# A two-layer mixer and mixture-of-experts kernel on Trainium2: block-ordered tokens at the second layer's hand-over

## The chip, the cores and the metric

One core of one Trainium2 chip runs the whole program in one launch. The metric is device time in microseconds (us), the median of several runs. Engines are named as in the profile: PE is TensorE, DVE is VectorE, ACT is ScalarE, POOL is GpSimd, SP is SyncE, which here only issues DMAs.

## What is computed

Two layers run over 256 tokens and 256 context tokens of width 1024 in float32. Each has a token mixer, an output projection, a layer norm, and a mixture of 16 experts of which every token uses two. In the second layer the context drops out, and only the 256 tokens go through the experts.

```python
y, yc = mixer(h, hc, w_in[l], ...)
x = layer_norm(alpha * x + g1 * y, ln1_g[l], ln1_b[l])
h2 = x * (1.0 + sc2) + sh2
f = moe(h2, w_router, router_bias, w_gate[l], w_up[l], w_down[l])
x = layer_norm(alpha * x + g2 * f, ln2_g[l], ln2_b[l])

def moe(h, ...):
    s = sigmoid(h @ w_router)          # 16 scores a token
    ...                                # best group of four experts, best two in it
    for e in range(16):
        y = y + gates[:, e:e+1] * ((silu(h @ w_gate[e]) * (h @ w_up[e])) @ w_down[e])
```

## The kernel before

Tokens stand on partitions, 128 to a block. In the second layer there are two blocks, `tb` 0 and 1. A row of 1024 features is split for a contraction into 8 groups of 128. The weights are laid out so that feature p * 8 + k lies on partition p in group k; a token's row is therefore seen as `t (p k)`, and group k of it is read in steps of 8 numbers (32 bytes).

**Order of the work.** Each engine has one queue. The build framework fills the queues from the order of the code, from priorities and from data dependences; `behind` and `seq` (a dependence without a semaphore) pin some neighbours by hand, and `hold` names the last instruction of ACT and of DVE behind which later work has to stay. Buffers are rotated: a load waits until the readers of its buffer are done.

**The hand-over of the second layer** lies between the output projection (`outproj`, line 727) and the first expert (`experts1`). These are its steps:
- `ln1` (line 776) takes the projection's sums, adds the residual, and keeps the result in `zs`, with the mean and the reciprocal root of the variance aside. `trans` and `logits` turn `zs` on PE and multiply it by the router's weights. `cent` (line 837) subtracts the mean and multiplies by the row `V["A2"]`; `norm` (line 841) multiplies by the root and adds `V["B2"]`. Their result is `h2`, in tile C. `keep` is true in the second layer: `h2` stays in memory and isn't written out.
- `part` (line 899, called in two steps for each block) splits `h2` into three bf16 pieces `hp` in tile A whose sum is the float32 value: a cast on ACT, the rest on DVE, a second cast on ACT, and the rest of the rest on DVE. In the kernel before, `h2` is ordered `t (p k)` and the pieces `t k p`, so each step reads `h2` in steps of 32 bytes; the first rest overwrites `h2`.
- `score` (line 1365) turns the router's sums into scores (a sigmoid on ACT), ranks them on DVE, and ends in `chb`, the chosen experts as zeros and ones (line 1417). `route` counts them on PE with the constant tiles `tri` and `one` (lines 1434 and 1438), and derives positions; `onehot` (line 1930) makes the selecting matrices `oh`, and `sort` orders the experts by load and writes their numbers, `eid`.
- `hgather` (line 1942) gathers the tokens of the first expert with 48 bf16 matmuls of the pieces and `oh`. ACT copies the result, and then the experts run back to back on PE: `gu` (gate and up), `dn` (down), `acc` (the sum).

The experts' weights come as pieces of 1 MB through SP's queue into a ring of 17 buffers (`wload`, line 1762). For the later experts SP first loads `eid` into registers (`expert`, line 1775). From its first free buffer on, the ring is refilled as PE gives pieces up.

**The modulation rows.** `vectors` (line 656) makes four rows `md`: 0 is g1, 1 is A2, 2 is B2, 3 is g2; ACT writes them to DRAM as `vd` with one DMA, and SP reads them back spread over all partitions (`vload`, line 689) into `V`.

## Time and profile before

| | us |
|---|---|
| median of 3 runs (lowest to highest) | 1177.66 (1174.02 to 1183.37) |
| profiled execution | 1171.57 |
| its span, first to last instruction | 1169.7 |
| PE busy in the span | 1066.6 (91%) |
| DVE busy | 745.1 (64%) |
| ACT busy | 526.5 (45%) |
| POOL busy | 127.7 (11%) |

The profile is of one execution. Its times count from the first instruction. A row of the chain gives a piece of work that the end of the program waited for; a row of the timeline gives every instruction, whether waited for or not; a row of the windows gives for a stretch how long each engine was busy, the clock that TensorE was granted (1.00 is 2.4 GHz, 0.50 is 1.2 GHz) and what the 16 DMA engines moved. "Idle before" is what an engine waited for.

### The profile page before, as it was taken

The numbers are of one execution on the slowest core, as the hardware profiler recorded it, in microseconds if no ns is written. First come the engines' busy times: TensorE is split into PE (matmuls) and PEld (weight loads), VectorE is DVE, ScalarE is ACT, GpSimd is POOL, SyncE is SP. The second block draws the span as 40 slices with busy tenths as digits, with TensorE's granted clock in tenths as the row PEclk, the third lists the DMA queues.
The fourth block names the chain that finished last, engine by engine and source line by source line (L and its number), as shares of the span: only waits on it lengthen the run. The fifth ranks groups of instructions, "written<-read, shape, count | busy, mean of one in ns | idle before, by whom it ended". The sixth has DMA issues, their size and how long they took to land.

```text
span 1169.7 us, 18719 instructions
## 1 busy us (share of the span) xinstructions
PE 1066.6 (91%) x7041; PEld 696.0 (60%) x7041; DVE 745.1 (64%) x1703; ACT 526.5 (45%) x872; POOL 127.7 (11%) x136
## 2 busy tenths in 40 slices
PE   5999999999994999999999868999999499999992
PEld 3766766665684777677543468667657345544441
DVE  3456687768689999788623685678786932222224
ACT  2363443437553778588633454543555511111112
POOL 0000011100000134344320000101100000000000
PEclk9999999999996999999999989999999599999996
DMA  9757666653376899799999941645539389999992
GB/s 378 274 211 260 251 231 234 232 187 145 109 271 213 299 354 360 273 356 392 368 406 415 409 155 72 232 165 180 181 121 344 138 345 423 420 422 423 421 422 96
DMA packets 55202, 327.14 MB, mean 280 GB/s; under 512 B 9467, under 2 KB 9723, under 8 KB 19776
## 3 DMA queue, kind: packets, MB, share of 16 engines
q1 hardware_dynamic: 44080, 275.60, 60.9%
q0 software_dynamic: 9152, 50.10, 11.6%
q8 instruction: 57, 0.93, 0.3%
q10 hardware_dynamic: 1872, 0.16, 0.1%
q14 instruction: 41, 0.34, 0.1%
HBM read 316.53 MB, written 13.09 MB: 282 GB/s over the span
## 4 chain that ended last, share of the span: by engine, by line
PE 49%; DVE 7%; ACT 3%; issue 2%; DMA 1%; POOL 1%; DVEq 0%; ACTq 0%; POOLq 0%
PE gu L185 9%; PE gu L1647 6%; PE proj L432 6%; PE dn L185 4%; PE dn L1647 4%; PE gu L1638 4%; PE hgt L185 2%; PE acc L185 2%; PE dn L1638 2%; PE op L727 2%; DMA G<-in_w_ada_dram 1%; PE hgt L1597 1%; PE S L1117 1%; PE pt L1140 1%; PE py L1147 1%
## 5 line engine op out<-in xcount | busy, mean ns | idle before, releaser
L294 ACT CAST T<-G 128x1024 fp32r<-128x1024 f32 (+2 forms) x79 | 78.1, 994 | 83.9 <-PE proj L432 56.2
L294 ACT CAST S<-G 128x1024 fp32r<-128x1024 f32 (+2 forms) x83 | 79.3, 958 | 79.0 <-PE proj L432 51.5
L304 DVE TENSOR_TENSOR S<-G,S 128x1024 fp32r<-128x1024 f32 (+2 forms) x75 | 85.2, 1140 | 41.4 <-ACT S L294 39.6
L185 PE MATMUL gu<-G,C 128*64 128x512 f32 (+2 forms) x608 | 107.8, 501 | 0.7 <-ACT C L1620 0.7
L304 DVE TENSOR_TENSOR T<-G,T 128x1024 fp32r<-128x1024 f32 (+2 forms) x69 | 82.3, 1198 | 39.7 <-ACT T L294 39.1
L432 PE MATMUL proj<-A,T 128*128 128x512 f32 (+1 forms) x336 | 97.2, 363 | 1.5 <-ACT T L294 1.0
L432 PE MATMUL proj<-A,S 128*128 128x256 f32 (+1 forms) x336 | 88.5, 342 | 1.3 <-DVE S L304 0.9
L1970 DVE SCALAR_TENSOR_TENSOR vt<-dn,slot,con 128x512 f32<-128x512 f32 x17 | 12.8, 751 | 98.6 <-PE dn L185 98.5
L185 PEld LDWEIGHTS gu<-G,C 128*64 128x64 f32 (+2 forms) x608 | 37.6, 128 | 56.7 <-issue 47.5
L432 PEld LDWEIGHTS proj<-A,T 128*128 128x128 f32 x336 | 59.7, 189 | 16.7 <-issue 4.6
L432 PEld LDWEIGHTS proj<-A,S 128*128 128x128 f32 x336 | 58.2, 190 | 11.5 <-issue 3.1
L1971 ACT CAST S<-vt 128x512 fp32r<-128x512 f32 x17 | 10.5, 618 | 98.8 <-DVE vt L1970 98.8
L1647 PE MATMUL gu<-C,A 128*128 128x512 f32 (+3 forms) x180 | 49.7, 408 | 1.2 <-DVE C L304 1.2
L1647 PE MATMUL gu<-T,A 128*128 128x512 f32 (+3 forms) x174 | 47.6, 402 | 3.4 <-POOL T L302 2.2
L404 POOL DMA_DIRECT2D G<-in_w_ada_dram x40 | 21.9, 548 | 258.0 <-PE ada L411 164.7
L185 PE MATMUL dn<-G,A 128*64 128x512 f32 (+2 forms) x224 | 46.8, 594 | 0.4 <-ACT A L1620 0.4
L1590 POOL DMA_INDIRECT G<-h2d,idx x16 | 22.2, 1386 | 216.5 <-DVE oh L1574 138.7
L294 ACT CAST C<-G 128x1024 fp32r<-128x1024 f32 x38 | 39.8, 1047 | 12.8 <-PE gu L1647 8.0
L1129 ACT ACTIVATE G<-G,nm 128x512 f32<-128x512 f32 x48 | 34.4, 718 | 21.3 <-DVE nm L1127 10.8
L1638 PE MATMUL gu<-G,C 128*64 128x512 f32 x192 | 43.0, 595 | 0.0
L989 DVE TENSOR_TENSOR G<-G 128x256 f32<-128x256 f32 x112 | 42.6, 417 | 0.6
L411 PE MATMUL ada<-G,sT 128*32 128x256 f32 x640 | 40.3, 383 | 2.1 <-DMA G<-in_w_ada_dram 2.0
(477 smaller groups left out, 2387.2 us busy)
## 6 DMA issues: line engine op xcount, KB each, us to landing
G<-in_w_gate_dram SPq DMA_DIRECT2D x62, 1024.0 KB, 12.6
G<-in_w_up_dram SPq DMA_DIRECT2D x60, 1024.0 KB, 8.0
G<-in_w_down_dram SPq DMA_DIRECT2D x60, 1024.0 KB, 11.0
G<-in_w_ada_dram POOLq DMA_DIRECT2D x40, 1024.0 KB, 7.6
G<-in_w_in_dram SPq DMA_DIRECT2D x22, 1024.0 KB, 8.7
G<-in_w_out_dram SPq DMA_DIRECT2D x12, 1024.0 KB, 6.7
G<-in_w_ada_dram SPq DMA_DIRECT2D x8, 1024.0 KB, 15.9
G<-vd SPq DMA_DIRECT2D x11, 512.0 KB, 3.8
```

The costliest lines, as they stand in the source:

```text
L185: return self._then(self.b.nc.tensor.matmul(*a, **k))
L294: self.lasts = [self.nc.scalar.copy(hi, raw)]
L304: self.lasts.append(sub(lo, raw, v))
L404: self.late(nc.gpsimd.dma_start(t, self.ap["w_ada"][l, 4 * s + q]))
L411: nc.tensor.matmul(pb[g:g + 32, i * 256:(i + 1) * 256], self.sT[:, kb, :], w[i][:, kb * 256:(kb + 1) * 256], start=kb < 4, stop=kb >= 4, t ...
L432: self.nc.tensor.matmul(pb[:, t], a[:, c], m, start=first and n == 0 and i == 0, stop=last and n == len(kbs) - 1 and i == 2)
L727: nc.tensor.matmul(pbs[tb][h], a, w[j][h], start=n == 0 and i == 0, stop=n == KB - 1 and i == 2)
L989: mul = lambda o, v: tt(o, o, v.to_broadcast([P, n, c]), op=OP.mult)
L1129: nc.scalar.activation(Pt, Pt, AF.Exp, scale=-1.0, bias=m, accum_out=ls[:, i:i + 1])
L1590: self.lastg = nc.gpsimd.indirect_dma_start(out=hg[:cap], out_offset=None, in_=h2d[:, :], in_offset=bass.IndirectOffsetOnAxis(ap=ig, axis= ...
L1638: self.pe.matmul(pb[t], h[0][:, g + i], w[o // PIECE][:, o % PIECE:o % PIECE + 512], start=g == 0, stop=g + m == nk, tile_position=(0, i * ...
L1647: nc.tensor.matmul(pbs[j][:cap], h[a][:, k], ws[b][:, c], start=k == 0 and q == 0, stop=k == nk - 1 and q == 2)
```

## The change

`cent` and `norm` now make `h2` in the order `t (k p)`, block by block: `cent` reads `zs` in steps of 32 bytes and writes a contiguous row. For this the rows A2 and B2 are written to `vd` in that order, row by row (four DMAs from ACT instead of one). `part` then works on contiguous rows; the rest goes into a tile of its own (`rest`, in S) instead of over `h2`, and block 0's last subtraction moves from DVE to GpSimd. The calls of `part` move forward: block 0's second step into `ln1`, block 1's first step behind `norm(1)` in `score`, block 1's second step to the top of `route`. Last, PE gets 18 matmuls of the constant tile `one` (bf16, 512 columns) behind the last router matmul; nothing reads their result.

```diff
--- before.py
+++ after.py
@@ -44,6 +44,7 @@
 SPLITC = 6
 FILLS = ((4, 5, 4, 1), (3, 2, 1, 0))
 EARLY = 6
+WARM = 18
 TAILS = (4, 2)
 BANKS1 = {"gu": "d", "hgt": "d", "dn": "m", "hT": "m", "sl": "m"}
 ACC = "mmmd"
@@ -192,6 +193,12 @@
     def __init__(self, tc, ap, out, dbg=None, caps=CAPS):
         self.pe = tc.nc.tensor
         self.tc, self.nc, self.ap, self.out, self.dbg, self.caps = tc, tc.nc, ap, out, dbg or {}, caps
+
+    def warm(self, n, after):
+        out = self.bank("warm").rearrange("p (a b) -> p a b", a=4)
+        for _ in range(n):
+            i = self.nc.tensor.matmul(out, self.one, self.one[:, None, :].to_broadcast([P, 4, P]), start=True, stop=True)
+            self.behind(i, after)
 
     def dump(self, name, t):
         if name in self.dbg:
@@ -683,8 +690,14 @@
             nc.tensor.matmul(pv[:, :, c], self.onef, rb[:, :, c], start=True, stop=True)
         nc.vector.tensor_copy(self.rb[:, :, :n], pv[:, :, :n])
         self.vd = self.dram([8, D], f"vd{l}")
+        vd = self.vd[:, :].rearrange("(r c) (p k) -> p r c k", c=2, k=KB)
+        if l == DEPTH - 1 and not self.general:
+            turned = self.vd[:, :].rearrange("(r c) (k p) -> p r c k", c=2, k=KB)
+            for r in range(4):
+                nc.scalar.dma_start((turned if r in (1, 2) else vd)[:, r, 0], md[:, r, 0])
+            return
         for c in range(n):
-            nc.scalar.dma_start(self.vd[:, :].rearrange("(r c) (p k) -> p r c k", c=2, k=KB)[:, :, c], md[:, :, c])
+            nc.scalar.dma_start(vd[:, :, c], md[:, :, c])
 
     def vload(self, dst, row):
         self.late(self.nc.sync.dma_start(dst, row.to_broadcast([P, D])))
@@ -830,11 +843,16 @@
 
         def logits(tb, hT):
             for kb in range(KB):
-                nc.tensor.matmul(lg[:, tb * NE:(tb + 1) * NE], hT[:, kb * P:(kb + 1) * P], self.wA[:, c, kb, :],
-                                 start=kb == 0, stop=kb == KB - 1)
+                i = nc.tensor.matmul(lg[:, tb * NE:(tb + 1) * NE], hT[:, kb * P:(kb + 1) * P], self.wA[:, c, kb, :],
+                                     start=kb == 0, stop=kb == KB - 1)
+            return i
 
         def cent(tb):
-            return stt(h2[tb], zs[tb], col(nmu, gs[tb]), V["A2", c], op0=OP.add, op1=OP.mult)
+            o, i, m = h2[tb], zs[tb], V["A2", c]
+            if keep:
+                o, m = (v.rearrange("t (k p) -> t k p", k=KB) for v in (o, m))
+                i = i.rearrange("t (p k) -> t k p", k=KB)
+            return stt(o, i, col(nmu, gs[tb]), m, op0=OP.add, op1=OP.mult)
 
         def norm(tb):
             g = gs[tb]
@@ -853,16 +871,21 @@
             square(1)
             hT1 = trans(1)
             logits(0, hT)
-            logits(1, hT1)
+            i = logits(1, hT1)
+            if keep:
+                self.warm(WARM, i)
             va.append(self.rsqrt(col(vs, 1), col(rstd, gs[1]), roots[1]))
             va.append(cent(1))
             if keep:
                 hp = [self.region("A", F32)[:, j * (D // 2):(j + 1) * (D // 2)].bitcast(BF16).rearrange("t (k p) -> t k p", k=KB)
                       for j in range(6)]
                 self.hp = [hp[0:3], hp[3:6]]
+                r1 = self.region("S", F32)
+                self.rest = [r1[:, j * D:(j + 1) * D] for j in range(2)]
                 a, v = self.part(0, h2[0], 0)
                 aa.append(a)
                 va.append(v)
+                aa.append(self.part(0, h2[0], 1)[0])
             aa.append(nc.scalar.activation(self.st("sg", 1), col(nmu, gs[1]), AF.Sigmoid))
             self.hold = [self.seq(*aa), self.seq(*va)]
         else:
@@ -889,7 +912,12 @@
         if final:
             self.res = res
             self.h2 = h2
-            self.score(l, c, lambda: norm(1))
+            def between():
+                norm(1)
+                if keep:
+                    self.part(1, h2[1], 0)
+
+            self.score(l, c, between)
         else:
             self.score(l, c)
             yield
@@ -897,9 +925,11 @@
         yield
 
     def part(self, tb, h, i):
-        v = h.rearrange("t (p k) -> t k p", k=KB)
+        v, r = (u.rearrange("t (k p) -> t k p", k=KB) for u in (h, self.rest[tb]))
         p = self.hp[tb]
-        return self.nc.scalar.copy(p[i], v), self.nc.vector.tensor_sub(v if i == 0 else p[2], v, p[i])
+        if i == 0:
+            return self.nc.scalar.copy(p[0], v), self.nc.vector.tensor_sub(r, v, p[0])
+        return self.nc.scalar.copy(p[1], r), (self.nc.vector if tb else self.nc.gpsimd).tensor_sub(p[2], r, p[1])
 
     def evict(self, l, c, pb):
         nc = self.nc
@@ -1427,8 +1457,7 @@
         tt = nc.vector.tensor_tensor
         pp = self.bank("pos")
         if l == DEPTH - 1 and not self.general:
-            self.part(0, self.h2[0], 1)
-            self.part(1, self.h2[1], 0)
+            self.part(1, self.h2[1], 1)
         for tb in range(B):
             for o in range(tb + 1):
                 nc.tensor.matmul(pp[:, tb * NE:(tb + 1) * NE], self.tri if o == tb else self.one, chb[:, o],
@@ -1506,7 +1535,6 @@
         posr = self.posr = self.st("posr", 4 * NE, bufs=1)[:, :B * N].rearrange("p (b e) -> p b e", b=B)
         if l == DEPTH - 1:
             self.hold[1] = self.onehot(l, 0)
-            self.part(1, self.h2[1], 1)
             sort()
             gates()
             tt(w[:, 0], w[:, 0], den[:, :, None].to_broadcast([P, B, NE]), op=OP.mult)
```

Line numbers of the changed kernel are some 7 to 30 higher than those of the kernel before.

DVE, from the second `norm` to the comparisons of the ranking. Tile C is `h2`, A the pieces, S the new rest, `vt` and `cmp` scratch of the ranking. Before:

```order
L841 SCALAR_TENSOR_TENSOR C<-C,st_7407,G 128x1024
L1399 TENSOR_TENSOR vt<-rs,s_rbias 128x32
L902 TENSOR_TENSOR A<-C,A 128x1024
L1401 TENSOR_TENSOR vt<-vt 128x8x3
L1402 TENSOR_TENSOR vt<-vt 128x8x2
L1403 TENSOR_TENSOR vt<-vt 128x8
L902 TENSOR_TENSOR C<-C,A 128x8x128
L1404 TENSOR_REDUCE vt<-vt 128x8
L1488 MEMSET vt 128x1 x2
L1409 TENSOR_TENSOR cmp<-vt 128x160
L1410 TENSOR_TENSOR cmp<-vt 128x160
```

After, at the same place:

```order
L859 SCALAR_TENSOR_TENSOR C<-C,st_7410,G 128x1024
L1429 TENSOR_TENSOR vt<-rs,s_rbias 128x32
L1517 MEMSET vt 128x1 x2
L1431 TENSOR_TENSOR vt<-vt 128x8x3
L1432 TENSOR_TENSOR vt<-vt 128x8x2
L1433 TENSOR_TENSOR vt<-vt 128x8
L1517 MEMSET vt 128x1
L1518 MEMSET vt 128x13
L1434 TENSOR_REDUCE vt<-vt 128x8
L1439 TENSOR_TENSOR cmp<-vt 128x160
L931 TENSOR_TENSOR S<-C,A 128x1024
L1440 TENSOR_TENSOR cmp<-vt 128x160
```

Block 0's last subtraction (A<-C,A) is gone from DVE, block 1's first (now S<-C,A) stands one comparison later, and four memsets come earlier.

ACT, from the first cast to the copy of the gathered tokens. The sigmoid of the scores is `rs<-rs`. Before:

```order
L902 CAST A<-C 128x1024
L866 ACT_TABLE_LOAD
L866 ACTIVATE sg<-st_7407 128x1
L902 CAST A<-C 128x1024
L1391 ACTIVATE rs<-rs 128x32
L902 CAST A<-C 128x1024 x2
L1620 COPY C<-hgt 128x512
```

After, at the same place:

```order
L931 CAST A<-C 128x1024
L932 CAST A<-S 128x1024
L889 ACT_TABLE_LOAD
L889 ACTIVATE sg<-st_7410 128x1
L1421 ACTIVATE rs<-rs 128x32
L931 CAST A<-C 128x1024
L932 CAST A<-S 128x1024
L1648 COPY C<-hgt 128x512
```

The second cast of block 0 now stands ahead of the table load and of the scores' sigmoid, where it stood behind both.

SP, in the second layer's mixer (`vd` read as rows g1 and A2). Before:

```order
L266 DMA G<-in_w_in_dram 128x2048 x6
L1771 DMA G<-in_w_gate_dram 128x2048
L266 DMA G<-in_w_in_dram 128x2048
L266 DMA G<-in_w_out_dram 128x2048 x3
L690 DMA G<-vd_6755 128x1024 x2
L266 DMA G<-in_w_out_dram 128x2048
```

After, at the same place:

```order
L273 DMA G<-in_w_in_dram 128x2048 x4
L703 DMA G<-vd_6755 128x1024 x2
L273 DMA G<-in_w_in_dram 128x2048 x2
L1799 DMA G<-in_w_gate_dram 128x2048
L273 DMA G<-in_w_in_dram 128x2048
L273 DMA G<-in_w_out_dram 128x2048 x4
```

The two reads of `vd` are now three loads of `w_in`, three of `w_out` and one of `w_gate` further ahead. In the first layer's output projection some instructions of PE, DVE and ACT change places, though no code of it is changed.

## Rows read from the trace of the kernel before

**Rows 1.** Windows: us; busy us (count) of PE, PEld, DVE, ACT, POOL; clock; DMA share; GB/s.

```profile
909.00:910.00 1.00, 1.00 (x10) 1.00 (x9) 0.96 (x2) 0.21 (x1) 0.00 (x0) 0.87 0.00 0
...
937.00:938.00 1.00, 1.00 (x6) 0.28 (x4) 1.00 (x4) 0.00 (x0) 0.00 (x0) 0.98 0.00 0
...
1000.00:1050.00 50.00, 50.00 (x344) 24.72 (x338) 10.46 (x32) 7.61 (x14) 0.00 (x0) 1.00 1.01 421
```

**Rows 2.** Chain that ended last, from 880 us on: start, us, what.

```profile
905.92 1.28 DVE C L837
...
913.15 2.00 ACT A L902
...
915.18 2.04 DVE C L902
...
928.50 0.18 DVE chb L1417
...
929.72 2.73 PE hgt L1942 x48
...
933.16 8.99 PE gu L185 x32
...
948.29 3.58 PE gu L185 x16
...
958.74 1.51 PE hgt L185 x48
...
1145.78 1.97 PE dn L185 x16
```

**Rows 3.** Timeline of the pause: start, us, engine, line, operation, tiles, shapes [idle].

```profile
905.37 0.39 PE L727 MATMUL op<-T,A 128*128 128x512 f32 x1
...
912.46 3.60 PE L833 MATMUL lg<-wA,B 128*128 128x16 f32 x16
...
912.90 1.28 DVE L837 SCALAR_TENSOR_TENSOR C<-G,st 128x1024 f32<-128x1024 f32 x1
...
915.17 1.28 ACT L866 ACT_TABLE_LOAD   x1
...
917.67 1.29 DVE L841 SCALAR_TENSOR_TENSOR C<-C,st,G 128x1024 f32<-128x1024 f32 x1
...
919.21 0.22 ACT L1391 ACTIVATE rs<-rs 128x32 f32<-128x32 f32 x1
...
919.46 0.19 DVE L1399 TENSOR_TENSOR vt<-rs,s_rbias 128x32 f32<-128x32 f32 x1 [0.49 <-ACT rs L1391]
...
925.80 1.99 DVE L902 TENSOR_TENSOR A<-C,A 128x1024 bf16<-128x1024 f32 x1 [0.96 <-ACT A L902]
```

**Rows 4.** Line 294, casts into S: ns min/median/max, first and last start, forms.

```profile
L294 ACT CAST S<-G x83: 398/1048/1074, 15.3 to 897.2; 128x1024 fp32r<-128x1024 f32 x71, 128x256 fp32r<-128x256 f32 x11, 128x512 fp32r<-128x512 f32 x1
```

**Rows 5.** Timeline of the first layer's experts, DVE and POOL.

```profile
411.72 1.33 POOL L302 TENSOR_TENSOR S<-G,S 128x512 fp32r<-128x512 f32 x1 [1.07 <-ACT S L294]
...
411.83 2.30 DVE L304 TENSOR_TENSOR T<-G,T 128x1024 fp32r<-128x1024 f32 x1
...
414.13 1.21 DVE L304 TENSOR_TENSOR C<-G,C 128x1024 fp32r<-128x1024 f32 x1
```

**Rows 6.** Line 302, GpSimd's subtractions into S.

```profile
L302 POOL TENSOR_TENSOR S<-G,S x8: 1274/1950/2320, 411.7 to 553.8; 128x512 fp32r<-128x512 f32 x8
```

**Rows 7.** SP: the loads of expert numbers, and the first weight load after them.

```profile
L1777 SPq TENSOR_LOAD <-eid x8: 263/268/278, 933.1 to 937.5; - x8
...
938.76 0.34 SPq L1771 DMA_DIRECT2D G<-in_w_down_dram  x1
```

**Rows 8.** DMA issues of 1122 to 1124 us: count, KB each, us to landing.

```profile
G<-in_w_down_dram SPq DMA_DIRECT2D x1, 1024.0 KB, 19.7
```

**Rows 9.** Line 667, the products that make row A2; and w_in loads of 775 to 795 us.

```profile
L667 DVE TENSOR_TENSOR md<-g,s_lnv x2: 166/177/188, 112.1 to 752.8; 128x16 f32<-128x16 f32 x1, 128x8 f32<-128x8 f32 x1
...
L266 SPq DMA_DIRECT2D G<-in_w_in_dram x2: 328/328/328, 776.6 to 791.9; - x2
```

## Prediction

> **What bounds the kernel now.** I read the windows first, then the chain of waits, then the timeline of the stretch in which the chain leaves PE, and last the waits of SP's queue. The chain shows PE nearly everywhere; the exception that this change touches is the pause between the router's matmuls, which end at 912.46 + 3.60 = 916.06 us [rows 3], and the first expert's gate at 933.16 [rows 2]. In it the chain goes through the first centring (905.92), a cast (913.15, 2.00 us), a subtraction (915.18, 2.04), the scores, more casts and subtractions, `chb` (928.50 to 928.68), the gather (929.72, 2.73) and a copy. Every step of the split stands there with about 2.0 us [rows 2, 3]. The clock falls between 909 and 910 (its mean is 0.87: full for 0.74 us, so the fall is at 909.74), 4.0 us after the last projection matmul (905.37 + 0.39 = 905.76), and is back up at 937.0, 3.9 us after the gate began [rows 1 to 3]. The gather takes 2.73 us at 1.2 GHz against 1.51 later at 2.4 GHz, the gate 8.99 for 32 matmuls against 3.58 for 16 [rows 2].
>
> From then on two things run side by side to the end: PE without a gap, and DMA at a share of 1.01 and 421 GB/s [rows 1]. The refill starts late because SP reads eight expert numbers first, from 933.1 to about 938.0 (the last of eight starts at 937.5, 0.6 us apart); its first load goes out at 938.76, when PE also has freed a buffer [rows 7]. At the end the DMA is only just ahead: the last down piece but one, issued at 1122.0, lands 19.7 us later at 1141.7 [rows 8]; the next follows one 2.8 us later (1 MB takes 2.5 us at 421 GB/s), and the matmuls that need it begin at 1145.78, its half about 1 us later [rows 2]. That is some 2.3 us of slack.
>
> **The change, step by step.** I replay the pause from 905.92 with new durations.
>
> The centring now reads in steps of 32 bytes. No row shows this operation so; the bounds are 1.28 us, its present price [rows 2], and 2.04, the dearest strided operation of that size [rows 2]. I take 2.0, since the subtractions of the same size read the same way: +0.7 us on the chain for block 0, and all behind it is late by this. In return a cast falls from 2.0 to 1.05 [rows 4], and a subtraction from 2.0 to 1.21 [rows 5].
>
> Block 0: the cast runs from 913.87 to 914.9. The second centring, 912.90 [rows 3] plus 0.7, ends at 915.6 and is late next; the subtraction follows to 916.8. Before, it ended at 917.2: only 0.4 us are won here. The four small score operations take what they took between 917.2 and 917.67 [rows 3], and `norm(1)` runs 917.3 to 918.6. On ACT the second cast now goes first (916.8 to 917.9), and the table load of 1.28 us [rows 3], which stood hidden under the first subtraction, follows it: the sigmoid ends at 919.5 instead of 919.4. So up to the scores nothing is won at all.
>
> GpSimd's subtraction: its inputs are there at 917.9. The nearest rows are halves of this size, 1.27 to 2.32 us [rows 6]; doubled, 2.5 to 4.6. I take 2.6, twice the uncontended 1.3. What it does to DVE is seen in the first layer: a GpSimd half runs 411.72 to 413.05, and the DVE subtraction that starts at 411.83 takes 2.30 us, not the 1.21 of the next one; it ends 1.08 after GpSimd does [rows 5]. DVE stood still for as long as GpSimd ran. Here GpSimd begins when `norm(1)` lets it, at 918.6, and ends at 921.2; the ranking's first addition (before at 919.46 [rows 3]) is ready at 919.6 and loses 1.6 us. The Trainium skill ("SBUF — State Buffer", section "SBUF: two separate sides") has the rule that speaks against the change: a GpSimd operation and a DVE operation with two SBUF inputs exclude each other for a whole instruction. Rows 5 agree; by the opposite view, that work moved to an idle engine is free, the sum would be 1.6 us better, which is a rival below.
>
> From the addition to the end of `chb` before: 919.46 to 928.68 are 9.2 us, of which three subtractions of 2.0 and a wait of 0.96 for ACT [rows 3] are 6.9; 2.3 are small operations. Now two subtractions remain (2.4), and ACT's cast of 1.05 lies beside the comparisons: 921.2 + 2.3 + 2.4 = 925.9. **`chb` comes 2.8 us sooner.** Positions, `oh` and `eid` keep their order behind it.
>
> The 18 matmuls start at 916.06 + 0.7 = 916.8. No row has their size; 48 matmuls of 64 columns took 2.73 and 1.51 us [rows 2], 57 and 31 ns each, so 512 columns are an estimated 0.46 at 1.2 GHz and 0.25 at 2.4: 4.5 to 8.2 us in all. With the clock up 3.9 us after they begin, it is 3.9 + 2.4 = 6.3, to 923.1; even the upper bound ends at 925.0, before `chb`. They delay nothing. What they bring hangs on the clock holding until the gather at 926.9. The fall before came 4.0 us after dense work [rows 1, 3]; that would be 927.1 here, about the moment when the gather begins, and the rise may come sooner or later than it did at the gate. This is close to a toss-up. I take it that it holds: the gather costs 1.5, not 2.7 (−1.2), the gate begins at 933.16 − 4.0 = 929.2 and takes 7.0 instead of 9.0. PE is then 6.0 us ahead.
>
> The refill gains less. SP needs `eid` (2.8 sooner) and its eight reads, to 935.2; its first load leaves at 935.3, 3.5 us sooner. The weights' stream is full to the end, so its end moves by 3.5, and PE can use that plus the slack of 2.3: 5.8. **The end moves by 5.5 us** (between the two, a little less for small losses).
>
> At nothing I cost the DMAs of `vd`. A2's products are made at 752.8, and the read of A2 now stands on SP ahead of the w_in load of 776.6 [rows 9], so the write has some 20 us to land. In its new order each element is a run of 4 bytes, for which there is no row; if it took longer than that cover, SP's queue would hand each further us to the w_in loads behind the read. The moved instructions in the first layer are the same work in another order on a busy PE: 0, give or take 1.5 us.
>
> Sum: 1171.57 − 5.5 = 1166.1 for an execution like the profiled one. That execution is 6.1 us under the median of 1177.66, so I forecast **1172.2 us**, −0.5%.
>
> **Rivals.**
> - *The clock is down again when the gather comes.* For it: the 4.0 us above; against: the fall before came after a stretch of transposes and small matmuls, not in a free one, so the spacing isn't known well. Then −2.8 remains, PE and refill alike: 1174.9.
> - *DVE isn't held up*, because GpSimd's piece falls between DVE's operations. For it: DVE idles from 918.6 to 919.6; against: rows 5. Then `chb` is 4.4 sooner, PE with the clock 7.6, the refill 4.9 plus slack 7.2: 1170.5.
> - *GpSimd is slow with bf16.* Place: DVE between the scores and the ranking, and the gather, which needs this piece. No row shows GpSimd with bf16 operands. At twice the slowest float32 row, 9.3 us, it ends at 927.9, `chb` at 932.6, 4.0 later than now, the clock is lost again: 1181.7. It decides from 5.4 us of the subtraction on without the clock's gain, from about 8.6 with it. Against: every GpSimd half of this kind took at most 2.32 [rows 6].
> - *The 18 matmuls leave the clock unmoved,* or the clock rises and falls before use: the first rival's number.
>
> **How the numbers follow.** Forecast 0.42, first rival 0.30, second 0.14, third 0.09, the rest (first layer's order, `vd` late) 0.05. All but the third lie below the old median, and all within 1% of it, which is about what a measurement of this kernel can tell from no change. The range holds the first three cases, 1170.5 to 1174.9, and as the three runs of before differ by up to 9 us, 5 us on either side: 1165.5 to 1180. Faster by over 1% would need 11.8 us; the whole pause is 17 us and no sum above gives it without the spread of the runs: 0.10. Slower by over 1% needs more than the third rival or a stall of the queues: 0.04.
>
> **What would show it.** Right: the contiguous casts at 1.05 and subtractions at 1.2; the centring at 2.0; one DVE addition behind the scores stretched until GpSimd's subtraction ends; `chb` about 12.6 us after the router's matmuls before, 9.1 after; the granted clock at 1.00 during the first gather, which takes 1.5; eight register reads, not PE, ahead of the first refill. Wrong: a gather of 2.7 and a gate of 9 (first rival), an addition that isn't stretched (second), a GpSimd piece beyond 5 us (third), PE waiting for weights at the end by more than the shift allows, or a w_in load later than its buffer.

## Result and the profile after

| us | before | after |
|---|---|---|
| median, same chip, 7 runs each | 1174.00 | 1186.66 |
| lowest to highest | 1170.52 to 1183.37 | 1184.89 to 1196.23 |
| profiled execution | 1171.57 | 1196.23 |
| its span | 1169.7 | 1194.2 |

The ratio is 1.0119, with a 95% interval of 1.0097 to 1.0142: about 1.2% slower, where 1172.2 us and a range up to 1180 were forecast. Of the experiments below, one execution of run 9 and one of the kernel before beside it took 2074 and 4524 us and are left out of the ratios. The profiled execution of after is the slowest of its seven, so its rows overstate the loss, by some 10 us against the median.

To find the place, I laid SP's loads of the two profiles side by side, since SP has the same loads in both, but for the earlier place of the two reads of `vd`: a load of `w_in` ahead of the second layer's mixer, the gate load in the middle of its mixer, the gate load at the start of its output projection. Before:

```profile
680.94 111.27 SPq L266 DMA_DIRECT2D G<-in_w_in_dram  x6
803.36 0.33 SPq L1771 DMA_DIRECT2D G<-in_w_gate_dram  x1
...
864.81 0.33 SPq L1771 DMA_DIRECT2D G<-in_w_gate_dram  x1
```


After:

```profile
687.44 75.74 SPq L273 DMA_DIRECT2D G<-in_w_in_dram  x4
778.51 0.82 SPq L703 DMA_DIRECT2D G<-vd  x2
...
826.51 0.33 SPq L1799 DMA_DIRECT2D G<-in_w_gate_dram  x1
...
893.34 0.33 SPq L1799 DMA_DIRECT2D G<-in_w_gate_dram  x1
```


The lag is 6.5 us, then 23.2, then 28.5. From there to the first centring it stays (864.81 to 905.92 is 41.1 us, 893.34 to 934.47 also), and at the end it is 24.5. So against the profile of before, the profiled run lost 6.5 us ahead of the first of these loads, 16.6 and 5.4 in the second layer's mixer, and won 4.1 in the hand-over. The 6.5 aren't all the change: the same load starts anywhere from 680.6 to 687.1 (mean 682.9) in the sixteen profiles of this study whose first layer has the order of before, and at 685.1, 686.5 and 687.4 in the three with the changed order.

**The pieces of the hand-over came as forecast.** Its timeline after answers to [rows 2, 3, 7]:

```profile
934.47 2.09 DVE L855 SCALAR_TENSOR_TENSOR C<-G,st 128x1024 f32<-128x1024 f32 x1
...
937.77 3.40 PE L846 MATMUL lg<-wA,B 128*128 128x16 f32 x16
...
943.33 2.14 DVE L855 SCALAR_TENSOR_TENSOR C<-G,st 128x1024 f32<-128x1024 f32 x1
...
945.39 1.21 DVE L931 TENSOR_TENSOR S<-C,A 128x1024 f32<-128x1024 f32 x1
...
946.32 6.56 PE L200 MATMUL warm<-one 128*128 128x512 bf16 x18
...
947.76 2.60 POOL L932 TENSOR_TENSOR A<-S,A 128x1024 bf16<-128x1024 f32 x1 [79.10 <-ACT A L932]
...
949.35 1.07 DVE L1429 TENSOR_TENSOR vt<-rs,s_rbias 128x32 f32<-128x32 f32 x1 [0.96 <-ACT rs L1421]
...
955.12 0.18 DVE L1447 CAST chb<-rc 128x32 bf16<-128x32 f32 x1
...
956.32 1.57 PE L1970 MATMUL hgt<-oh,A 128*128 128x64 bf16 x48 [0.70 <-DVE oh L1958]
...
958.63 7.09 PE L186 MATMUL gu<-G,C 128*64 128x512 f32 x32 [0.73 <-ACT C L1648]
...
964.68 0.34 SPq L1799 DMA_DIRECT2D G<-in_w_down_dram  x1
```


And its windows (columns as in [rows 1]):

```profile
938.00:940.00 2.00, 2.00 (x11) 2.00 (x11) 1.90 (x7) 0.72 (x2) 0.00 (x0) 0.50 0.00 0
...
950.00:952.00 2.00, 2.00 (x7) 0.77 (x6) 1.94 (x11) 0.25 (x1) 0.37 (x1) 0.64 1.01 426
952.00:954.00 2.00, 0.88 (x5) 0.29 (x3) 1.90 (x8) 1.05 (x1) 0.00 (x0) 1.00 1.01 426
...
956.00:958.00 2.00, 1.57 (x48) 1.48 (x48) 2.00 (x7) 0.01 (x1) 0.00 (x0) 1.00 0.01 4
```


The centring takes 2.09 us instead of 1.28, GpSimd's piece 2.60, and the DVE addition beside it 1.07 instead of 0.19. The constant matmuls (`warm`) take 6.56 and end at 952.88, the clock is back at 1.00 by then, and the gather takes 1.57 instead of 2.73, the gate 7.09 instead of 8.99. Counted from the start of the first centring, `chb` comes at 20.6 (before 22.6), the gate at 24.2 (27.2), the first refill at 30.2 (32.8), the end at 259.7 (263.8).

**The mixer lost the time.** The waits of PE from 700 to 905 us have a new first row (us in total, times, longest; before: 0.2 us, once):

```profile
PE ada L418 <- DMA G<-in_w_ada_dram: 11.6, 2, 7.8
```


The timeline shows the longer of the two:

```profile
760.92 0.37 ACTq L697 DMA_DIRECT2D vd<-md  x1
...
763.76 0.53 POOL L411 DMA_DIRECT2D G<-in_w_ada_dram  x1 [4.51 <-PE ada L418]
763.82 0.28 PE L439 MATMUL proj<-B,S 128*128 128x256 f32 x1
...
771.94 1.94 PE L418 MATMUL ada<-G,sT 128*32 128x256 f32 x16 [7.84 <-DMA G<-in_w_ada_dram]
...
774.21 0.53 POOL L411 DMA_DIRECT2D G<-in_w_ada_dram  x1 [9.92 <-PE ada L418]
```

The windows of the same stretch, columns as before:

```profile
755.00:760.00 5.00, 5.00 (x35) 3.48 (x36) 0.00 (x0) 0.59 (x1) 1.06 (x2) 1.00 0.67 226
760.00:764.00 4.00, 4.00 (x39) 2.21 (x38) 3.82 (x12) 2.41 (x4) 0.24 (x1) 1.00 0.86 255
764.00:772.00 8.00, 0.16 (x5) 0.06 (x8) 2.16 (x5) 0.00 (x0) 0.29 (x1) 0.70 0.73 40
772.00:774.00 2.00, 2.00 (x17) 0.73 (x18) 0.00 (x0) 0.00 (x0) 0.00 (x0) 0.50 0.54 94
774.00:778.00 4.00, 4.00 (x15) 2.33 (x15) 0.38 (x2) 1.87 (x2) 0.53 (x1) 0.58 0.89 365
```


At 760.92 ACT issues the write of A2. PE's product of the modulation (`ada`, line 418) waits for a `w_ada` load until 771.94, and the projection's matmuls behind it in PE's queue wait too. From 764 to 772 the 16 DMA engines move 40 GB/s, and the compute engines stand nearly still. The DMA view of these 8 us (packets, MB, share of the 16 engines' time) shows that the write itself is over:

```profile
q1 hardware_dynamic: 39, 0.32, 72.8%
q10 hardware_dynamic: 65, 0.00, 0.5%
q0 software_dynamic: 1, 0.00, 0.0%
```


Of its 1040 packets (q10) 65 are left, which are gone by 764.4 and take 0.5% of the engines' time. The 39 packets of the `w_in` load (q1) take 72.8% of 16 x 8 us, 2.4 us each, and of the `w_ada` loads (q0) one single packet moves. In the kernel before, the packets of `w_in` took 0.35 us each from 755 to 775:

```profile
q1 hardware_dynamic: 144, 1.05, 15.8%
```

So the loads behind the write crawl after its last packet has gone. The Trainium skill ("DMA: Bandwidth & Descriptors", section "Rules for kernel authors") says that a strided last dimension becomes one descriptor per element. The 1040 packets agree: they are 1024 elements and 16 more, and a write of the same row in 128 runs of 32 bytes (run 4) has 144.

The waits are 11.6 of the 16.6 us. Most of the rest is the clock, which fell in the stall (0.50 from 768 to 774). From the `w_in` load at 680.94 or 687.44 to the gate load at 803.36 or 826.51, PE has the same 839 matmuls in both kernels (columns as before; before, then after):

```profile
680.94:803.36 122.42, 112.57 (x839) 88.11 (x839) 88.63 (x221) 58.80 (x104) 10.96 (x19) 0.99 0.43 155
687.44:826.51 139.07, 118.23 (x839) 91.84 (x839) 88.72 (x221) 58.80 (x104) 10.98 (x19) 0.92 0.45 144
```

They take 118.2 us instead of 112.6.

The 5.4 us between 845 and 893 are of another kind: the clock was 0.52 from 862 to 876, and 1.00 in the same stretch before (839 to 853; after, then before):

```profile
862.00:876.00 14.00, 12.95 (x43) 8.79 (x44) 9.77 (x34) 6.16 (x17) 3.01 (x4) 0.52 0.00 1
```

```profile
839.00:853.00 14.00, 13.02 (x78) 8.80 (x80) 13.12 (x44) 8.96 (x24) 3.01 (x4) 1.00 0.10 40
```

Of the nineteen profiles of this study twelve show such a fall there (45.6 to 49.4 us between the first `w_out` load and the gate load, 43.2 in the other seven), the kernel before among the seven. Neither the change nor its writes decide it (run 8 has both and shows no fall, run 13 has neither and does), so I count it with the spread of some 10 us that every kernel has. One tie is left open: all six kernels that turn A2 and B2 on PE (runs 5, 6, 7, 11, 12, 13) are among the twelve, and only six of the other thirteen; with one profile each, this may be chance.

### The profile page after: what moved, and what is told of

Same layout as the page of the kernel before. It is cut to its first block, busy times and chain, and to the rows that moved or that the text cites. A ratio compares the mean times of both kernels' runs of the same rounds, so it can differ in the third digit from the quotient of the medians.

```text
span 1194.2 us, 18761 instructions
## 1 busy us (share of the span) xinstructions
PE 1088.1 (91%) x7059; PEld 709.7 (59%) x7059; DVE 742.8 (62%) x1702; ACT 523.3 (44%) x872; POOL 130.3 (11%) x137
## 4 chain that ended last, share of the span: by engine, by line
PE 72%; DVE 14%; DMA 5%; ACT 4%; issue 3%; POOL 1%; SPq 0%; ACTq 0%; DVEq 0%; POOLq 0%
PE proj L439 12%; PE gu L186 8%; PE gu L1675 7%; PE dn L186 4%; DMA G<-in_w_ada_dram 4%; PE op L740 4%; PE dn L1675 4%; PE gu L1666 4%; PE first L439 3%; PE ada L418 2%; PE pt L1170 2%; PE hgt L186 2%; PE dn L1666 2%; PE acc L186 2%; PE S L1147 2%
## 5 line engine op out<-in xcount | busy, mean ns | idle before, releaser
L439 PE MATMUL proj<-A,S 128*128 128x256 f32 (+1 forms) x336 | 91.3, 351 | 1.3 <-DVE S L311 0.9
## 6 DMA issues: line engine op xcount, KB each, us to landing
G<-in_w_down_dram SPq DMA_DIRECT2D x60, 1024.0 KB, 11.6
```

What stands on the lines that cost most here:

```text
L439: self.nc.tensor.matmul(pb[:, t], a[:, c], m, start=first and n == 0 and i == 0, stop=last and n == len(kbs) - 1 and i == 2)
```

## Experiments

Ratios are to the kernel before on the same chip, over 6 to 12 executions each against 23 to 35 of before (medians 1174.7 to 1176.6). They are taken over the executions themselves, and differ from the quotient of the two medians by up to 0.2%. One per cent is 11.7 us. Each kernel has one profile.

| run | kernel | median, us | ratio (95%) |
|---|---|---|---|
| 1 | change, one write in 32-byte runs | 1174.37 | 1.0002 (0.9983 to 1.0021) |
| 2 | change, four writes in 32-byte runs | 1180.27 | 1.0057 (1.0031 to 1.0082) |
| 3 | before + two writes in 4-byte runs | 1186.15 | 1.0079 (1.0051 to 1.0107) |
| 4 | before + two writes in 32-byte runs | 1174.64 | 0.9998 (0.9978 to 1.0018) |
| 5 | change, A2 and B2 reordered on PE | 1177.78 | 1.0012 (0.9991 to 1.0033) |
| 6 | 5 with 30 constant matmuls | 1174.04 | 0.9987 (0.9970 to 1.0004) |
| 7 | 5 with none | 1179.49 | 1.0024 (1.0006 to 1.0041) |
| 8 | change, rows 0 and 3 joined | 1183.43 | 1.0061 (1.0036 to 1.0086) |
| 9 | 3, writes 75 and 106 us later | 1177.13 | 1.0007 (0.9987 to 1.0027) |
| 10 | 3, runs 64 bytes apart | 1178.79 | 1.0036 (1.0012 to 1.0059) |
| 11 | 6, last subtraction on DVE | 1174.82 | 0.9996 (0.9975 to 1.0016) |
| 12 | 6, centring later | 1173.81 | 0.9995 (0.9977 to 1.0013) |
| 13 | before + run 5's transposes | 1177.94 | 1.0012 (0.9993 to 1.0032) |
| 14 | 1, centring later, 30 matmuls | 1174.02 | 0.9989 (0.9967 to 1.0011) |
| 15 | before, centring later | 1174.79 | 1.0013 (0.9991 to 1.0035) |
| 16 | before, row 0 written early | 1179.08 | 1.0023 (1.0000 to 1.0046) |
| 17 | before + 42 constant matmuls | 1175.29 | 0.9990 (0.9972 to 1.0009) |

### The 4-byte writes: runs 3, 4, 9, 10

```diff
+ex = self.dram([2, D], "ex")[:, :].rearrange("r (k p) -> p r k", k=KB)   # run 3; run 4: (p k)
+for r in range(2):
+    nc.scalar.dma_start(ex[:, r], md[:, 1 + r, 0])
```

Every queue stands as before, with two DMAs more on ACT; nobody reads the two rows.

> The kernel before and nothing of the change, with two more writes from ACT's queue: rows A2 and B2 of md, in runs of 4 bytes, to two scratch rows of memory that nobody reads. Theory (4-byte runs): 15 us slower than the kernel before (8.5 to 10 from the first write, 5 from the second), about 1189; PE waits twice for w_ada, together about 11 us. Rival (order of the queues): within 1 us of the kernel before, since nobody waits for the two writes.

> As the run before, but the two additional writes go out in runs of 32 bytes (128 runs each instead of 1024). Theory (4-byte runs): within 1 us of the kernel before. Rival (any additional write of small runs into the stretch of the w_ada loads costs it): 4 us or more slower.

Run 3 is 0.8% slower, some 9 us of the 15 expected; run 4 is the same as before. The waits of PE in run 3's second mixer:

```profile
PE ada L411 <- DMA G<-in_w_ada_dram: 5.3, 2, 5.1
```

Its windows behind the two writes, columns as in [rows 1] (then the kernel before in two of the stretches):

```profile
758.00:762.00 4.00, 4.00 (x35) 2.10 (x27) 2.65 (x8) 1.96 (x3) 0.53 (x1) 1.00 0.48 23
...
790.00:794.00 4.00, 0.29 (x8) 0.00 (x0) 3.07 (x9) 0.69 (x2) 0.54 (x1) 1.00 0.12 14
```

```profile
758.00:762.00 4.00, 4.00 (x26) 2.58 (x25) 2.64 (x9) 2.32 (x4) 0.37 (x1) 1.00 1.02 403
...
790.00:794.00 4.00, 4.00 (x34) 3.15 (x30) 3.79 (x13) 0.59 (x1) 0.55 (x1) 1.00 0.84 279
```


The stretch from that `w_in` load to that gate load (122.4 us in the kernel before) separates the profiles: it takes 131.5 us in run 3, 131.4 in run 8 and 139.1 in the changed kernel, which have neighbouring 4-byte runs in it, and 122.3 to 124.7 in the other sixteen. So in this place the writes in 4-byte runs alone cost 0.5 to 1.1%. Two writes of the same bytes in 32-byte runs cost nothing that 12 executions can tell. These two runs don't say whether the length of the runs or their number (1024 or 128 a row) does it.

Run 9 issues the writes of run 3 where no load is in flight (a dependence without a semaphore puts them behind a cast of the output projection):

> The kernel before with the two additional 4-byte writes of the third run, but issued some 50 to 90 us later, at about 850 us, between the landing of the last w_out load (about 841) and the next load (864.8), when the trace of the kernel before moves no data. Theory (the writes cost time because the w_ada loads behind which PE waits are in flight with them): within 1.5 us of the kernel before. Rival (they cost what they cost wherever they stand, through ACT's queue or their landing): 8 to 11 us slower, as in the third run.

The DMA queue of the two writes in run 9, from 858 to 876 us (packets, MB, share):

```profile
q10 hardware_dynamic: 2080, 0.01, 5.2%
```


The 2080 packets go out (the writes start at 860.1, the next load at 876.2), and the time is that of the kernel before within its interval: it isn't the write by itself that costs, but what it does to loads that it meets and that PE waits for.

Run 10 spreads the runs:

```diff
-ex = self.dram([2, D], "ex")[:, :].rearrange("r (k p) -> p r k", k=KB)
+ex = self.dram([2, 16 * D], "ex")[:, :].rearrange("r (k p s) -> p r k s", k=KB, s=16)[:, :, :, 0]
```

> The third run (kernel before, two additional writes of 1024 runs of 4 bytes at their places), but each run of 4 bytes goes 64 bytes behind the last instead of next to it. Theory A (the number of small writes is what holds up the loads): as the third run, 8 to 11 us slower. Theory B (that neighbours in memory are written one after the other, the reads behind them waiting): under 2 us slower. The trace of the changed kernel speaks for B: the 1040 packets of the write were gone by 764.4, and the loads crawled at 17 to 94 GB/s until 773.

The waits of PE in run 10:

```profile
PE ada L411 <- DMA G<-in_w_ada_dram: 1.1, 2, 0.9
```


The stall is nearly gone from the trace (1.1 us of waits instead of 5.3; 248 and 406 GB/s from 758 to 766 instead of 23 and 27), with the same number of packets, and the stretch from the `w_in` load to the gate load takes 124.7 us, within the sixteen. That speaks for neighbours that hold each other up (Theory B). But the time, some 4 us over before, lies between the two theories, and its interval touches neither 1.000 nor run 3's middle. So the mechanism isn't settled.

### The order that comes with four DMAs: runs 1, 2, 8, 16

```diff
 if keep:   # cent; norm likewise
-    o, m = (v.rearrange("t (k p) -> t k p", k=KB) for v in (o, m))
-    i = i.rearrange("t (p k) -> t k p", k=KB)
+    o = o.rearrange("t (k p) -> t k p", k=KB)
+    i, m = (v.rearrange("t (p k) -> t k p", k=KB) for v in (i, m))
 # run 2: for r in range(4): nc.scalar.dma_start(vd[:, r, 0], md[:, r, 0]);  run 1: the one DMA of before
```

> The changed kernel, but vd is written as before (one DMA with 32-byte runs, A2 and B2 in their old order), and the centring and both norms read A2 or B2 in steps of 32 bytes instead. Theory (the two writes in 4-byte runs hold up the w_ada loads; the hand-over itself gained 4 us): 4 us under the kernel before, about 1170 where that gives 1174; PE waits for w_ada for under 1 us in all between 700 and 905 us, and the chain from the first centring to the gather is as in the changed kernel. Rival (four DMAs and the earlier reads of vd on SP's queue cost the time, not the 4-byte runs): the same 1170, since these are gone too. Rival (the hand-over loses time, and the rest is chance of the clock): 1180 or more.

> The changed kernel with its four DMAs for vd at their places, and every queue in the changed kernel's order, but all four rows written in 32-byte runs; the centring and both norms read A2 and B2 in steps of 32 bytes. Theory (4-byte runs): about 1170, and no wait of PE for w_ada over 1 us. Rival (the order of the queues, four DMAs instead of one): about 1186, as the changed kernel, with the late stretch between 763 and 780 us still there.

Run 1 won nothing against before, run 2 lost 0.6%, and the first theory had both at 1170. That PE waits for `w_ada` under 1 us in both (0.3 and 0.4) is as expected; so the 4-byte runs aren't all. Run 2 has every queue in the order of the changed kernel. Its order differs from run 1's in the first layer, where row 0 of the second layer's `vd` now goes out, and on SP, where two reads of `vd` stand further ahead. Run 16 has the first of these, and one of the two reads (at 766.1 instead of 832.8):

```diff
+if l == DEPTH - 1 and not self.general:
+    nc.scalar.dma_start(vd[:, 0, 0], md[:, 0, 0])
+    nc.scalar.dma_start(vd[:, 1:4, 0], md[:, 1:4, 0])
+    return
```

> The kernel before, but row 0 of the second layer's vd goes out in a DMA of its own as soon as it is there, which is in the first layer, and rows 1 to 3 in another; all in 32-byte runs. PE, DVE and ACT then have the changed kernel's order in the first layer's attention and output projection, and the second layer is as before. Theory (this order costs the 3 to 6 us between run 2 and run 1): 3 to 6 us slower than the kernel before, the distance between the first two loads of the layer-norm rows 19.9 us instead of 18.7. Rival (the order is worth nothing, run 2 lost its time elsewhere): within 1.5 us.

SP's first two loads of layer-norm rows in run 16:

```profile
300.46 0.33 SPq L695 DMA_DIRECT2D G<-in_lnr_dram  x1
...
320.33 0.33 SPq L695 DMA_DIRECT2D G<-in_lnr_dram  x1
```


The 19.9 us between these loads, instead of 18.7, are in the profile of every kernel with this order (after, 2, 16), and in none of the others. The time is 0.2% up, with an interval from 0 to 0.5%: 2 to 3 us here, between theory and rival and at the edge of nothing; between run 1 and run 2 it was 5.9. Run 8 takes the early DMA out of the changed kernel and leaves the 4-byte writes:

```diff
-for r in range(4): nc.scalar.dma_start((turned if r in (1, 2) else vd)[:, r, 0], md[:, r, 0])
+for r in (1, 2): nc.scalar.dma_start(turned[:, r, 0], md[:, r, 0])
+nc.scalar.dma_start(vd[:, 0::3, 0], md[:, 0::3, 0])
```

> The changed kernel with A2 and B2 turned by 4-byte writes at their places, but rows 0 and 3 written together, so that no DMA of vd goes out in the first layer and its order is as before. Theory (three parts that add up: 4-byte runs +11, order of the first layer +6, hand-over -4): 7 us over the kernel before, about 1182. Rival (the order of the first layer costs nothing, the second run's +6 was from SP's early reads of vd, which stay for A2): about 1187.

1183.43 is near the theory's 1182 (its profiled execution, 1176.67, is one of its fastest). PE waits 7.3 us for `w_ada` there. The changed kernel has all that run 8 has, the order of the first layer, one early read on SP and one DMA besides: 1.0119 (1.0097 to 1.0142) to 1.0061 (1.0036 to 1.0086), 0.6%. So the order costs something, by 0.2 to 0.6%; no run parts it from the early read of row 0.

### What the hand-over is worth: runs 1, 5 to 7, 11 to 15, 17

Why run 1 won nothing is in its pause, here its timeline:

```profile
912.51 2.10 DVE L857 SCALAR_TENSOR_TENSOR C<-C,st,G 128x1024 f32<-128x1024 f32 x1
...
919.91 2.07 DVE L857 SCALAR_TENSOR_TENSOR C<-C,st,G 128x1024 f32<-128x1024 f32 x1
...
920.59 3.39 POOL L930 TENSOR_TENSOR A<-S,A 128x1024 bf16<-128x1024 f32 x1 [74.93 <-ACT A L930]
...
922.17 1.85 DVE L1427 TENSOR_TENSOR vt<-rs,s_rbias 128x32 f32<-128x32 f32 x1 [0.19 <-ACT rs L1419]
...
932.52 9.71 PE L186 MATMUL gu<-G,C 128*64 128x512 f32 x32 [0.73 <-ACT C L1646]
```


The norms, which now read B2 in steps of 32 bytes, take 2.07 instead of 1.28, the second collides with GpSimd (3.39 instead of 2.60), the addition takes 1.85, and the clock has fallen again when the gate comes: 9.71 instead of 7.09. So A2 and B2 were brought into the new order another way, by transposes on PE, and the number of constant matmuls was varied:

```diff
 # ... the four DMAs are one again; A2 and B2 are read back from self.vt
+for r in (1, 2): nc.tensor.transpose(pb[:KB, r * P:(r + 1) * P], md[:, r, 0], self.ident)
+t = self.st("tmp", 512)[:KB, :2 * P]
+nc.vector.tensor_copy(t, pb[:KB, P:3 * P])
+nc.scalar.dma_start(self.vt[:, :].rearrange("r (k p) -> k r p", k=KB), t.rearrange("k (r p) -> k r p", r=2))
-WARM = 18
+WARM = 30   # run 6; run 7: 0
```

> The changed kernel, but vd is written in one DMA as before, and A2 and B2 are turned on PE (two transposes of 128 x 8, one copy) and written a second time in runs of 512 bytes, from where the centring and the norms read them block by block. Now: 4-byte runs cost about 11 us (the third run against before), the order with four DMAs about 6 (the second run against the first), and the hand-over gains 4 where the clock holds to the gate, 0 where it falls (the first run: gate 9.71). Theory: norm back at 1.28, the clock at 1.00 through the gather, the gate at 7.1, 4 us under the kernel before, about 1171. Rival (that the clock held in the one profile of the changed kernel was chance): the gate at 9 or more and no more than 1 us under the kernel before.

> The run before with 30 constant matmuls instead of 18; 12 more at 0.22 to 0.25 us end about 2.8 us later, some 0.7 us ahead of the gather. [...] Rival (18 hold the clock only by chance): 30 are 2 to 4 us faster than 18. If the 30 reach past chb, the gather is late by as much and it is slower by up to 1 us.

> The same without the constant matmuls. Theory: the gather takes 2.7 us and the gate 9, PE is 3 us later at the gate's end, and the time is 2 to 4 us above the run with 18, so 1173 to 1175. Rival (the refill alone sets the end): within 1 us of the run with 18.

With 18 the gate takes 9.10, with none 9.83, with 30 7.09 and the gather 1.57. From the first centring to the end it is 260.8, 264.0 and 259.7 us, in the profile of before 263.8. Such a row differs between executions too: with the hand-over of before it is 261.3 to 264.2 (before, 3, 4, 9, 10, 13, 16), and from the first refill to the end alone the nineteen profiles take 229.5 to 232.6. Where the clock is up through gather and gate (after, 6, 8, 11), the changed hand-over takes 258.4 to 259.7, so some 4 us are won. Where it falls, run 5 keeps 3 of them (260.8), runs 1, 2 and 7 keep nothing (264.0 to 264.6). In the medians, 30 are 3.7 us faster than 18, as run 6's rival had it, and 5.4 faster than none. That 18 hold the clock, as in the profiles of after and of run 8, isn't certain, as run 5's rival had it.

Run 17 has constant matmuls and nothing else:

```diff
+i = logits(1, hT1)
+if keep: self.warm(42, i)
```

> The kernel before with 42 constant matmuls behind the router's, and nothing else of the change (casts, subtractions and centring as before); they end about 2 us ahead of the gather. Theory: the clock holds, gather 1.57 instead of 2.72, gate 7.09 instead of 8.99, so PE is 3 us ahead at the gate's end; the refill starts no sooner, so the end gains its slack of 2.3 us: 2 to 3 us faster. Rival (the end is set by the refill): within 1 us.

PE's timeline in its pause:

```profile
925.63 11.54 PE L199 MATMUL warm<-one 128*128 128x512 bf16 x42
...
939.60 1.96 PE L1951 MATMUL hgt<-oh,A 128*128 128x64 bf16 x48 [0.70 <-DVE oh L1939]
942.30 9.61 PE L185 MATMUL gu<-G,C 128*64 128x512 f32 x32 [0.73 <-ACT C L1629]
```


Here the last of the 42 matmuls ended 2.4 us ahead of the gather, the clock fell during the gather (1.96) all the same, and the gate took 9.61; the time is that of before. Constant matmuls don't make the clock certain. Over all profiles, the clock was up at the gate in five of ten with them (after, 6, 8, 11, 12) and in four of nine without (4, 10, 13, 16); at the gather in the same five and in none of the nine.

Run 11 is run 6 with

```diff
-(self.nc.vector if tb else self.nc.gpsimd).tensor_sub(p[2], r, p[1])
+self.nc.vector.tensor_sub(p[2], r, p[1])
```

> The sixth run (turned on PE, 30 constant matmuls) with block 0's last subtraction on DVE instead of GpSimd. Theory (prediction: DVE's addition stands still for as long as GpSimd runs into it, 0.85 us here, so GpSimd saves only 1.22 - 0.85): chb 0.4 us later than in the sixth run, time within 1 us of it. Rival (the subtraction on GpSimd is free): 1.2 us or more later.

The positions start 20.66 us after the first centring, 20.83 in run 6, and the time is that of before, as in run 6: no gain or loss by GpSimd's piece shows.

Run 12 is run 6, run 14 run 1 with 30 constant matmuls, and run 15 the kernel before, each with

```diff
-va.append(cent(0))
 front(1)
+va.append(cent(0))
```

> The sixth run with block 0's strided centring moved behind the four operations of the second block's front on DVE, so that its 2.1 us don't stand ahead of what PE waits for. Theory (in the changed kernel the centring's additional 0.8 us kept PE waiting 2.2 instead of 1.4 us, the clock fell before the first router matmuls, 2.32 to 3.40 us, and so they ended 1.9 us later than before, not 0.7): the second block's transposes come 2 us sooner, the first router matmuls take 1.9, the second end 2 to 3 us sooner after the first block's sums, and the end comes 1 to 2 us sooner. Rival (DVE, which has the same work in all, is the bound of the pause): the scores come at the same time and the end within 0.5 us.

Counted from the square of block 0 on ACT, which precedes both places of the centring, PE's wait ahead of the second block's transposes is gone and the first router matmuls take 2.40, but the second end at 11.5 (12.0 in run 6), the scores start at 14.3 (14.8), the first refill at 28.8 (29.1), and the end comes at 261.1 (259.8), so what was won is lost behind the refill. The rival holds for the scores: DVE has the same work ahead of them in any order. Run 15 says the same of the kernel before:

> The kernel before with block 0's (contiguous) centring behind the second block's front, nothing else. Theory (DVE's order ahead of the second block's transposes sets PE's wait): the wait falls from 1.39 us to about 0.1, the second router matmuls end 1.5 to 3 us sooner; behind them the chain of casts on ACT and DVE is as long as before, so the gate comes 1 to 2 us sooner, the time is 1 to 2 us less. Rival (DVE bounds the pause): within 0.5 us.

The wait is gone there too; the second router matmuls end at 10.6 (10.2), the end is at 263.6 (263.8), the time that of before. What is left is run 6: 4 us in its rows, 1.7 in the median. Run 13 adds run 5's transposes on PE to the kernel before, with a scratch row for `vt`:

> The kernel before with nothing of the change but the two transposes of 128 x 8 on PE, their copy on DVE and one more write to a scratch row nobody reads. Theory (these 0.4 us on PE and 0.4 on DVE ahead of the small matmuls after 830 us make the clock fall there): 3 to 5 us slower than the kernel before in the median, with 46 to 49 us between the first w_out load and the gate load at 865. Rival (the clock falls there by chance in any kernel): within 1.5 us in the median.

> The first run (one write in 32-byte runs, strided centring and norms, no transposes) with the centring of block 0 behind the second block's front and 30 constant matmuls. Theory (the hand-over gains what its rows show, and the transposes gave it back): from the first block's sums to the end 4 us less than the kernel before even with the norms' additional 0.8 us each, and 3 to 5 us faster in the median, about 1170. Rival (the end is set by something the hand-over doesn't move): within 1.5 us of the kernel before.

Run 13 is 2.6 us over before in the median, with an interval from -0.1 to +0.3%: between its two theories. If the transposes cost that, the medians of runs 6 and 7 roughly fit the rows: 4 won and nothing won, and some 2.5 lost; run 11's, the same as before, fits less well. But an interval as wide as the effect doesn't show it. Run 14, which has no transposes but the slower norms, and a gate of 9.00 in spite of its 30 constant matmuls, wins 1.1 in its rows and 1.3 in the median, as its rival had it. No run is faster than before by more than its interval; no version here beats it.

## Why the prediction was wrong

**The step that failed** is "At nothing I cost the DMAs of `vd`". It looked only at whether the write lands in time for its own read in SP's queue. It did not ask what else is in flight on the same DMA engines and who waits for that. A run of 4 bytes had no row, so bounds were due, and the range had none for it. What the runs showed instead: the loads that the write meets crawl, and PE waits for them. Run 3 measures it alone: 0.8% (0.5 to 1.1), 9 us. In the profiled execution it was 16.6.

**The second step** is "0, give or take 1.5 us" for the first layer's order. With one early read on SP it measured 0.2% (0 to 0.5) in run 16, 2 to 3 us, and 0.6% between run 8 and the changed kernel, as between runs 1 and 2. "The same work in another order on a busy PE" took the busy share for proof that order is free.

**The hand-over** was right in its pieces: centring 2.09 (2.0 forecast), casts 1.05, subtractions 1.21 and 1.22, GpSimd 2.60 (2.6), constant matmuls 6.56 (6.3), gather 1.57 (1.5), gate 7.09 (7.0). The stretched addition lost 0.9 (1.6 forecast), which agrees with the prediction's rule on DVE and GpSimd (the Trainium skill, "SBUF — State Buffer", section "SBUF: two separate sides"). Two sums were off. "Up to the scores nothing is won at all" was too good: the router's matmuls ended 1.9 us later, and the scores' addition began 1.35 later. The two centrings put 1.6 us more on DVE, and DVE bounds this stretch (runs 12 and 15); PE waited 2.20 us for it instead of 1.39, and the clock fell before the first router matmuls, which took 3.40 instead of 2.32. So `chb` was 1.9 sooner, not 2.8, the refill 2.6, not 3.5, and the end 4.1, not 5.5. That the clock holds was called a toss-up, which runs 1, 2 and 5 bear out; that it held in the profile of after was luck. The other side had 2.8 us left in the first rival: run 5 keeps 3.0, run 7 nothing.

**The rivals.** The second (DVE isn't held) and the third (GpSimd at 5.4 us or more) were refuted by 1.07 and 2.60. None named what the write does to other loads: a late `vd` and the first layer's order stood in the rest, with 0.05, and the slow side had 0.04.

**The sum from the runs**: 4-byte writes 0.8%, first layer 0.2 to 0.6%, hand-over 0 to -0.3%. The middle of these is 1.0%; 1.2% (1.0 to 1.4) was measured. How large the second and the third part are stays open within these bounds.

## What to carry to other kernels

Cost a DMA by the transfers that it meets as well as by its own landing: look at which loads are in flight when it is issued, and which engine has its queue behind them. Give a layout change to an engine that is made for it, or to the reader, before it is written to memory in single elements; where only 4-byte runs will do, issue them where no load is in flight that an engine will wait for. And a shorter stretch in one profile isn't a gain until more executions show it, above all where a clock that comes and goes is worth as much.

## What the runs showed of the hardware that was not expected

- Two writes of 4 KB in 4-byte runs (run 3) kept 16 DMA engines at 14 to 61 GB/s for about 8 us each; in the changed kernel it was 40 GB/s for 8 us after nearly all of the write's own packets had ended. The same bytes in 32-byte runs did nothing that can be seen, and 4-byte runs 64 bytes apart little.
- PE's granted clock fell to 0.5 in the same stretch of small matmuls, between 842 and 876 us, in twelve profiles and stayed at 1.00 in seven, also among kernels whose order up to there is that of before (fell: 3, 9, 10; stayed: 4, 15). That is 2.4 to 6.2 us of a time of 1175. In the seven, the profiled execution is at or under the median of its kernel.
- Matmuls that nobody reads ended with the clock up in each of the ten profiles that have them, but didn't hold it: in run 17 the gather came 2.4 us behind them and the clock fell in its middle; in after the pause behind them was longer (952.9 to 956.3, with PE busy for 0.3 us) and the clock held. Without them the clock was up again when the gate began in four profiles of nine (4, 10, 13, 16).
